# Attention score block 0 and value block 3 run over 128 columns instead of 256

## The chip, the cores and the metric

The kernel runs on one core of a Trainium2 chip. The metric is the device time of one execution in microseconds (us), where lower is better. A core has a matrix engine (PE, with the loading of its stationary operand shown apart as PEld), a vector engine (DVE), a scalar engine (ACT), GpSimd (POOL), and SyncE (SP), which here issues DMA transfers. Every matmul writes to a bank of PSUM, 512 float32 columns wide, from which DVE or ACT take the result.

## The reference

Two layers of a decoder trunk at 512 tokens and width 1024. Each layer has three parallel branches (a Mamba-2 scan, latent attention, a gated delta net), a gated merge and a feed-forward part; a final norm follows. The change lies in the attention branch:

```python
kv = (rmsnorm(ckv, kv_norm_g) @ w_ukv).reshape(Bsz, S, H, MLA_NOPE + MLA_V)   # H = 8 heads
k_nope, v = jnp.split(kv, [MLA_NOPE], axis=-1)                                # 128 + 128
...
sc = (einsum('bqhd,bkhd->bhqk', qn, k_nope) + einsum('bqhr,bkr->bhqk', qp, k_pe))
qpos = blk * MLA_QBLOCK + jnp.arange(MLA_QBLOCK)                              # 4 blocks of 128 queries
sc = jnp.where(kpos[None, :] <= qpos[:, None], sc * scale, -jnp.inf)
pr = jax.nn.softmax(sc, axis=-1)
return einsum('bhqk,bkhd->bqhd', pr, v)
```

Attention is causal, so query block t sees keys of blocks 0 to t alone, and key block kb is seen by query blocks kb to 3 alone.

## The kernel before

Everything is in one function, `hybrid_kernel`, run under a framework that takes the instructions of the loops and places them on each engine's queue; the order on an engine is not that of the source, and a few places in the source raise a priority. Each engine works through its own queue in order and waits on semaphores for the others.

Matrix products are split in two: an operand in float32 becomes a high part (type float32r, rounded) and a low part (the rest, float32r too), and a product is three float32r matmuls, high by high, high by low and low by high (`mm3`, L198 to L202). Other products of the kernel, in the Mamba-2 and delta-net branches (L779, L873, L1053, L1070 and more), use plain float32 operands, and transposes (L686, L309) pass a float32 tile through PE with an identity matrix.

Attention runs in the loop over `hp` (L586): four pairs of heads in each layer, and within a pair `j` = 0, 1. So there are 4 x 2 x 2 layers = 16 passes of the inner code:

- **Scores** (L658 to L679). For each query block t, five float32r matmuls (L663 to L667) accumulate in one bank: three for the 128 non-rotary dimensions, two for the rotary ones. Their stationary operand is 128 x 128 (the queries), their moving operand is the keys, `n = max(256, (t + 1) * P)` columns wide: 256, 256, 384 and 512. A sixth matmul in bfloat16 (L668) adds the mask over the columns from `t * P` on. For t = 0 the second 128 columns are masked keys that nothing reads afterwards; L669 narrows `n` to 128 before DVE takes the row maximum (L672), ACT the exponential (L675, L676) and DVE normalises (L677, L678).
- **Values** (L680 to L706). The probabilities are transposed by key block (L686, ten transposes a head) and split into a high and a low part. Key blocks 0 and 1 give moving operands of 512 and 384 columns. Blocks 3 and 2 share one bank of transposes and one pair of tiles, `pts`: 128 columns of zeros (written once in each layer by POOL, L578), then 128 columns of block 3, then 256 of block 2. Block 2 multiplies the last 256 columns, block 3 the first 256, that is its own 128 and the 128 zeros, and adds the result to the last 256 columns of `po`. Each block takes three float32r matmuls (L702 to L704), with the values as stationary operand, 128 x 128.

The tiles of the attention stage lie in a pool `ml` that is closed after the loop; the pool `br` of the two other branches then takes its place. Products of the other branches (L200 to L202) and further weights stand on PE's queue between the pieces of attention.

Of the kernel before, what the change touches and what calls it, by code (L numbers as in the profile page):

```python
# [11 lines left out]
F32R = mybir.dt.float32r  # L12
# [8 lines left out]
P = 128  # L21
S = 512
# [33 lines left out]
def hybrid_kernel(ctx, tc, a, out, depth=2, taps=None):  # L56
# [4 lines left out]
    def mk(pl, shape, dt, tag, bufs=None):  # L61
        return pl.tile(shape, dt, tag=tag, name=f"{tag}_{next(uid)}", bufs=bufs)
# [5 lines left out]
    def f32(ap):  # L68
        return ap.bitcast(F32)
# [197 lines left out]
    def split_act(hi, lo, src):  # L267
        with tc.high_priority(30):
            act.copy(hi, src)
            dve.tensor_tensor(lo, src, f32(hi), ALU.subtract)  # L270
# [112 lines left out]
    for ly in range(depth):  # L383
# [189 lines left out]
        q_rs = mk(sp, [P, T], F32, "qrs")  # L573
        rsq(q_rs, ps[:, :T], 1.0 / 512, EPS)

        pts = [mk(ml, [P, S], F32R, f"pt{i}") for i in range(2)]
        for x in pts:
            pool.memset(f32(x[:, :P]), 0.0)  # L578

        qpl = [mk(ml, [P, S], F32R, f"qpl{j}") for j in range(2)]  # L580
        for j in range(2):
# [4 lines left out]
        for hp in range(4):  # L586
            def q_weights():
                for k0 in (0, 2):
                    raw = mk(wp, [P, 768], F32, "wraw", 2)
                    sync.dma_start(raw.rearrange("p (k n) -> p k n", k=2),  # L590
                                   a["mla_w_uq"][ly][k0 * P : (k0 + 2) * P, hp * 384 : (hp + 1) * 384].rearrange("(k p) n -> p k n", p=P))
                    for k in range(2):
                        rv = raw[:, k * 384 : (k + 1) * 384].rearrange("p (h n) -> p h n", h=2)
                        hi = mk(wp, [P, 384], F32R, "whi")
                        lo = mk(wp, [P, 384], F32R, "wlo")
                        nv = lambda x: x[:, :256].rearrange("p (h n) -> p h n", h=2)
                        pv = lambda x: x[:, 256:].rearrange("p (h n) -> p h n", h=2)
                        act.copy(nv(hi), rv[:, :, :P])
                        act.copy(pv(hi), rv[:, :, P:])
                        dve.tensor_tensor(nv(lo), rv[:, :, :P], f32(nv(hi)), ALU.subtract)  # L600
                        dve.tensor_tensor(pv(lo), rv[:, :, P:], f32(pv(hi)), ALU.subtract)
                        yield k0 + k, hi.unsqueeze(1), lo.unsqueeze(1)

            *pq, pp = dense_F(q_weights(), tiles(384), 512, cqh, cql, tag=(ly, "q", hp))

            def head_tiles(pss, nm, c=None):
                res = []
                for ps in pss:
                    hi = mk(ml, [P, S], F32R, nm + "h", 3)
                    lo = mk(ml, [P, S], F32R, nm + "l", 3)  # L610
                    if c is None:
                        split_act(hi, lo, ps)
                    else:
                        act.mul(hi, ps, c)
                        dve.scalar_tensor_tensor(lo, ps, c, f32(hi), ALU.mult, ALU.subtract)
                    res.append((hi, lo))
                return res

            qs = head_tiles(pq, "q", scale)
            qp = mk(ml, [P, S], F32, "qp")  # L620
            act.mul(qp, pp, scale)
            qr = rope(qp)

            qd = mk(lp, [P, S], F32, "mix", 8)
            for i in range(2):
                sync.dma_start(qd[64 * i : 64 * i + 64], qr[64 * (1 - i) : 64 * (1 - i) + 64])
            qps = [mk(ml, [P, S], F32R, f"qps{j}") for j in range(2)]
            for j in range(2):
                half, other = (slice(64 * i, 64 * i + 64) for i in (j, 1 - j))
                act.copy(qps[j][half], qr[half])  # L630
                dve.tensor_tensor(qpl[j][half], qr[half], f32(qps[j][half]), ALU.subtract)
                act.copy(qps[j][other], qd[other])
            wkv = list(weights(a["mla_w_ukv"][ly], hp * 512, 512, 256))
            with tc.high_priority(30):
                ks = head_tiles(dense_F(wkv, [slice(0, P), slice(256, 256 + P)], 256, ckh, ckl), "k")

            vs = []
            for j in range(2):
                if hp % 2 == 0:
                    v2 = [mk(ml, [P, S], F32R, nm, 2) for nm in ("vh", "vl")]  # L640
                elif hp == 1:
                    v2 = [mk(lp, [P, S], F32R, f"y{e}{6 + j}") for e in "hl"]
                else:
                    v2 = [mk(ml, [P, S], F32R, f"cq{e}{j}") for e in "hl"]
                vs.append([x.rearrange("p (t n) -> p t n", t=T) for x in v2])

            def ev(t, ps):
                for j in range(2):
                    split_act(*(x[:, t, :] for x in vs[j]), ps[:, j * P : (j + 1) * P])

            vcols = lambda w: w.rearrange("p (h n) -> p h n", h=2)[:, :, P:]
            dense_T(wkv, 256, 256, ckh, ckl, ev, vcols)

            for j in range(2):
                qh, ql = qs[j]
                kh, kl = ks[j]
                pn = []
                for t in range(T):  # L658
                    n = max(256, (t + 1) * P)
                    tok = slice(t * P, (t + 1) * P)  # L660
                    ps = sm_bank()
                    o = ps[:, :n]
                    pe.matmul(o, qh[:, tok], kh[:, :n], start=True, stop=False)  # L663
                    pe.matmul(o, qh[:, tok], kl[:, :n], start=False, stop=False)
                    pe.matmul(o, ql[:, tok], kh[:, :n], start=False, stop=False)
                    pe.matmul(o, qps[j][:, tok], kps[:, :n], start=False, stop=False)
                    pe.matmul(o, qpl[j][:, tok], kph[:, :n], start=False, stop=False)  # L667
                    pe.matmul(ps[:, t * P : n], id_b, am_b[:, : n - t * P], start=False, stop=True)  # L668
                    n = (t + 1) * P  # L669
                    o = ps[:, :n]  # L670
                    mx = mk(sp, [P, 1], F32, "mx", 8)
                    dve.tensor_reduce(mx, o, AX.X, ALU.max, negate=True)  # L672
                    pt_ = mk(ml, [P, (t + 1) * P], F32, f"pn{t}", 2)
                    sm = mk(sp, [P, 1], F32, "sme", 8)
                    act.activation(mx, mx, AF.Copy, scale=q_rs[:, t : t + 1])  # L675
                    act.activation(pt_[:, :n], o, AF.Exp, bias=mx, scale=q_rs[:, t : t + 1], accum_out=sm)  # L676
                    dve.reciprocal(sm, sm)  # L677
                    dve.tensor_scalar(pt_[:, :n], pt_[:, :n], sm, None, ALU.mult)  # L678
                    pn.append(pt_)  # L679
                po = y_bank()  # L680
                for kbs in ((0,), (1,), (3, 2)):
                    ps = sm_bank()
                    n = 0
                    for kb in kbs:
                        for t in range(kb, T):
                            pe.transpose(ps[:, n : n + P], pn[t][:, kb * P : (kb + 1) * P], ident)  # L686
                            n += P
                    if len(kbs) == 1:
                        th = mk(lp, [P, n], F32R, "mix", 8)
                        tl = mk(lp, [P, n], F32R, "mix", 8)  # L690
                        split_act(th, tl, ps[:, :n])
                        parts = [(kbs[0], kbs[0] * P, 0)]
                    else:

                        th, tl = pts
                        split_act(th[:, P:], tl[:, P:], ps[:, :n])
                        parts = [(2, 2 * P, 2 * P), (3, 2 * P, 0)]
                    for kb, c0, c in parts:
                        v_h, v_l = (x[:, kb, :] for x in vs[j])
                        o = po[:, c0:]  # L700
                        w = S - c0
                        pe.matmul(o, v_h, th[:, c : c + w], start=kb == 0, stop=False)  # L702
                        pe.matmul(o, v_h, tl[:, c : c + w], start=False, stop=False)
                        pe.matmul(o, v_l, th[:, c : c + w], start=False, stop=kb == T - 1)  # L704
                yh[2 * hp + j], yl[2 * hp + j] = (mk(lp, [P, S], F32R, f"y{e}{2 * hp + j}") for e in "hl")
                split_act(yh[2 * hp + j], yl[2 * hp + j], po)  # L706
                tap(f"oT{2 * hp + j}", f32(yh[2 * hp + j]))
            if hp == 0:
                dec, ndec, beta, dtq, dsk = step_sizes()
# [762 lines left out]
```

## Time and profile before

| | |
|---|---|
| runs | 2285.59, 2286.96, 2287.45 us, median 2286.96 us |
| span of the profiled execution, first to last instruction | 2283.0 us |
| around the span, against the median | 3.96 us |
| PE busy | 2260.8 us, 99% of the span, 11822 records |
| PEld busy (beside PE) | 1867.7 us, 82% |
| DVE, ACT, POOL busy | 1648.8, 1202.1, 64.9 us |
| mean granted PE clock | 0.999 of full speed |

The profiled execution has no device time of its own on the page beside its span. A row of a group gives line, engine, operation, output and inputs, shapes, count, then busy time and the mean duration of one in ns. A row of the timeline gives start and duration in us. Matmuls overlap in the pipeline: durations of neighbours overlap, so what a matmul costs is the distance from its start to the next one's, in a run where nothing waits. The attention stage of the first layer lies at about 60 to 190 us, that of the second at about 1230 to 1340 us.

### The profile page before, as it was taken

The page shows a single profiled execution, that of the slowest core. Times are in us where ns is not written, and L with a number is a line of the kernel's source. Part 1 is how long each engine was busy: PE and PEld are TensorE (multiplying, and loading weights), DVE is VectorE, ACT ScalarE, POOL GpSimd, SP SyncE. Part 2 cuts the span into 40 slices and gives each one's busy share as a digit, 9 for nine tenths or more (in the row PEclk, how much of TensorE's full clock was granted, in tenths as well). Part 3 has the DMA queues.
Part 4 walks back from the last instruction along what each step waited for, and adds up shares of the span by engine and source line. Part 5 has one row for each costly group of instructions (what it writes and reads, how often), then busy time and mean ns, then how long its engine had stood idle before and what let it go on. Part 6 is the DMA issues. An engine that isn't in the chain of part 4 may idle for free. (4 is left out here: it accounts for less than half of the span.)

```text
span 2283.0 us, 32306 instructions
## 1 busy us (share of the span) xinstructions
PE 2260.8 (99%) x11822; PEld 1867.7 (82%) x11822; DVE 1648.8 (72%) x3250; ACT 1202.1 (53%) x2508; POOL 64.9 (3%) x83
## 2 busy tenths in 40 slices
PE   9999999999999999999999999999999999999998
PEld 8888777888888888888888888788888887888886
DVE  7777567876667778767877775678757667778668
ACT  6766654333444465554657667443335445645545
POOL 1000000000000000000010000000001000000000
PEclk9999999999999999999999999999999999999999
DMA  4223634452224243233132236344422251432231
GB/s 145 81 74 102 192 99 122 115 157 75 84 74 166 65 148 107 90 100 119 47 104 81 71 110 198 98 121 140 129 76 83 65 178 44 166 111 99 86 111 47
DMA packets 220176, 244.23 MB, mean 107 GB/s; under 512 B 34272, under 2 KB 172528, under 8 KB 220016
## 3 DMA queue, kind: packets, MB, share of 16 engines
q1 hardware_dynamic: 220016, 242.16, 34.6%
q8 instruction: 93, 1.52, 0.3%
q14 instruction: 67, 0.55, 0.1%
HBM read 225.66 MB, written 11.74 MB: 104 GB/s over the span
## 5 line engine op out<-in xcount | busy, mean ns | idle before, releaser
L172 ACT CAST whi<-wraw 128x512 fp32r<-128x512 f32 (+1 forms) x536 | 329.4, 618 | 540.4 <-PE acc L201 365.0
L173 DVE TENSOR_TENSOR wlo<-wraw,whi 128x512 fp32r<-128x512 f32 (+1 forms) x536 | 365.3, 687 | 343.6 <-ACT whi L172 334.2
L200 PE MATMUL acc<-xh,whi 128*128 128x512 f32 (+1 forms) x1344 | 525.7, 392 | 0.2 <-ACT whi L172 0.2
L202 PE MATMUL acc<-xh,wlo 128*128 128x512 f32 (+1 forms) x1344 | 520.5, 388 | 0.0
L201 PE MATMUL acc<-xl,whi 128*128 128x512 f32 (+1 forms) x1344 | 520.3, 387 | 0.0
L202 PEld LDWEIGHTS acc<-xh,wlo 128*128 128x128 f32 x1344 | 252.5, 188 | 49.2 <-DVE wlo L173 0.4
L200 PEld LDWEIGHTS acc<-xh,whi 128*128 128x128 f32 x1344 | 252.5, 188 | 48.9 <-ACT whi L172 0.6
L201 PEld LDWEIGHTS acc<-xl,whi 128*128 128x128 f32 x1344 | 252.9, 188 | 47.3 <-DVE xl L274 0.7
L172 ACT CAST whi<-wr 128x512 fp32r<-128x512 f32 x168 | 104.3, 621 | 107.8 <-PE acc L201 47.6
L200 PE MATMUL acc<-yh,whi 128*128 128x512 f32 x384 | 152.2, 400 | 0.0
L201 PE MATMUL acc<-yl,whi 128*128 128x512 f32 x384 | 150.2, 391 | 0.0
L202 PE MATMUL acc<-yh,wlo 128*128 128x512 f32 x384 | 149.8, 390 | 0.0
L173 DVE TENSOR_TENSOR wlo<-wr,whi 128x512 fp32r<-128x512 f32 x168 | 113.3, 687 | 35.3 <-ACT whi L172 34.5
L727 DVE SCALAR_TENSOR_TENSOR ckl<-acc,pc,ckl 128x511 f32<-128x511 f32 (+2 forms) x168 | 121.2, 744 | 17.9 <-ACT ckl L723 10.6
L200 PEld LDWEIGHTS acc<-yh,whi 128*128 128x128 f32 x384 | 71.5, 188 | 16.5 <-ACT yh L273 2.3
L202 PEld LDWEIGHTS acc<-yh,wlo 128*128 128x128 f32 x384 | 72.1, 188 | 15.1
L201 PEld LDWEIGHTS acc<-yl,whi 128*128 128x128 f32 x384 | 72.2, 188 | 14.2
L200 PE MATMUL acc<-whi,xh 128*128 128x512 f32 (+1 forms) x208 | 79.7, 385 | 0.0
L201 PE MATMUL acc<-wlo,xh 128*128 128x512 f32 (+1 forms) x208 | 79.3, 381 | 0.0
L202 PE MATMUL acc<-whi,xl 128*128 128x512 f32 (+1 forms) x208 | 78.9, 382 | 0.0
L486 ACT ACTIVATE eE<-eE,cum 128x128 f32<-128x128 f32 x192 | 62.6, 391 | 30.8 <-DMA eE<-d_c 26.8
L1212 DVE TENSOR_TENSOR h<-h,acc 128x512 f32<-128x512 f32 x120 | 77.1, 681 | 0.1
(462 smaller groups left out, 4542.3 us busy)
## 6 DMA issues: line engine op xcount, KB each, us to landing
wraw<-in_w_in_dram SPq DMA_DIRECT2D x144, 512.0 KB, 3.6
wraw<-in_w_up_dram SPq DMA_DIRECT2D x64, 512.0 KB, 3.6
wr<-in_w_down_dram SPq DMA_DIRECT2D x32, 1024.0 KB, 5.0
eE<-d_c SPq DMA_DIRECT2D x48, 256.0 KB, 4.3
wraw<-in_w_mla_out_dram SPq DMA_DIRECT2D x16, 512.0 KB, 3.4
eE<-d_e SPq DMA_DIRECT2D x32, 256.0 KB, 3.0
wraw<-in_w_ssd_out_dram SPq DMA_DIRECT2D x16, 512.0 KB, 3.3
wraw<-in_w_gdn_out_dram SPq DMA_DIRECT2D x16, 512.0 KB, 3.3
```

Source lines behind the costliest of these rows:

```text
L172: act.copy(hi, raw)
L173: dve.tensor_tensor(lo, raw, f32(hi), ALU.subtract)
L200: pe.matmul(o, ah, bh, start=start, stop=False, skip_group_check=more)
L201: pe.matmul(o, ah, bl, start=False, stop=False, skip_group_check=more)
L202: return pe.matmul(o, al, bh, start=False, stop=stop, skip_group_check=more)
L486: act.activation(o[:, i], o[:, i], AF.Relu, scale=-1.0, bias=cum[:, t, h0 + i : h0 + i + 1])
L727: dve.scalar_tensor_tensor(acc[:, d:], ps[:, : S - d], taps_[3 - d], acc[:, d:], ALU.mult, ALU.add)
L1212: dve.tensor_tensor(hs_, hs_, ps[t], op)
```

## The change

The first query block's scores and the fourth key block's value product lose their 128 padded columns: `n` is 128 for t = 0, for the five score matmuls and the mask's; the tiles `pts` are 384 columns wide instead of 512 and need no zeros, so POOL's two memsets a layer go; block 3 multiplies its own 128 columns and adds them to the last 128 columns of `po`. What the other engines read and write is as before.

```diff
-        pts = [mk(ml, [P, S], F32R, f"pt{i}") for i in range(2)]
-        for x in pts:
-            pool.memset(f32(x[:, :P]), 0.0)
+        pts = [mk(ml, [P, S - P], F32R, f"pt{i}") for i in range(2)]
...
-                    n = max(256, (t + 1) * P)
+                    n = (t + 1) * P
...
-                    n = (t + 1) * P
-                    o = ps[:, :n]
                     mx = mk(sp, [P, 1], F32, "mx", 8)
...
-                        split_act(th[:, P:], tl[:, P:], ps[:, :n])
-                        parts = [(2, 2 * P, 2 * P), (3, 2 * P, 0)]
+                        split_act(th, tl, ps[:, :n])
+                        parts = [(2, 2 * P, P), (3, 3 * P, 0)]
```

## The prediction

> **What bounds the kernel.** I read the page's engine table first, then the busy times by stage, then who PE waits for.
>
> ```profile
> span 2283.0 us, 32306 instructions
> PE 2260.8 (99%) x11822; PEld 1867.7 (82%) x11822; DVE 1648.8 (72%) x3250; ACT 1202.1 (53%) x2508; POOL 64.9 (3%) x83
> ```
>
> PE has 22.2 us of idle time in the whole span. The stages of attention, and the stage right behind the first of them (columns: stretch, its length, then busy time of PE, PEld, DVE, ACT, POOL, PE clock, DMA):
>
> ```profile
> 60.00:190.00 130.00, 128.72 (x728) 106.42 (x727) 100.47 (x246) 89.89 (x242) 1.01 (x1) 1.00 0.26 73
> 1230.00:1340.00 110.00, 108.74 (x596) 89.09 (x595) 85.16 (x195) 75.70 (x192) 0.00 (x0) 1.00 0.29 83
> 190.00:230.00 40.00, 40.00 (x194) 32.79 (x193) 27.39 (x44) 25.75 (x54) 0.00 (x0) 1.00 0.41 119
> ```
>
> In the 240 us of attention PE is idle for 1.28 + 1.26 = 2.5 us, at full clock. Of all PE's waits, those of the attention stage are the last row and a few like it (waiting line, releasing line, us in total, times, longest):
>
> ```profile
> PE sm L752 <- DVE ft L282: 2.0, 2, 1.6
> ...
> PE sm L686 <- DVE pn L678: 1.2, 2, 0.6
> ```
>
> So in these stages time is PE time: what the change adds to or takes from PE's queue moves the end one for one, less at most 2.5 us that could vanish in waits. Everything turns on what a 128-column float32r matmul costs.
>
> **How many matmuls are cut.** One row for each kind, grouped by shape:
>
> ```profile
> L664 PE MATMUL sm<-kl,qh 128*128 128x256 f32 x32 | 9.0, 282 | 0.0
> L702 PE MATMUL yt<-pt,vh 128*128 128x256 f32 x16 | 4.5, 281 | 0.0
> L702 PE MATMUL yt<-pt,yh 128*128 128x256 f32 x8 | 2.3, 282 | 0.0
> L702 PE MATMUL yt<-pt,cqh 128*128 128x256 f32 x8 | 2.2, 280 | 0.0
> L668 PE MATMUL sm<-am_b,id_b 128*128 128x256 bf16 x16 | 4.5, 283 | 0.0
> ```
>
> A score line has 32 records of 256 columns, 16 for t = 0 and 16 for t = 1; the first half shrinks: 5 lines x 16 = 80. A value line has 16 + 8 + 8 = 32, half of them block 3: 3 lines x 16 = 48. Together **128 float32r matmuls** go from 256 to 128 columns, with 128 stationary columns before and after. The 16 mask matmuls shrink too.
>
> **What one costs now.** The value products of blocks 2 and 3 stand in one run (start, duration):
>
> ```profile
> 87.35 0.28 PE L702 MATMUL yt<-pt,vh 128*128 128x256 f32 x1
> ...
> 88.06 0.28 PE L666 MATMUL sm<-kps,qps 128*128 128x256 f32 x1
> ...
> 90.38 0.39 PE L664 MATMUL sm<-kl,qh 128*128 128x512 f32 x1
> 90.61 0.40 PE L665 MATMUL sm<-kh,ql 128*128 128x512 f32 x1
> 90.84 0.40 PE L666 MATMUL sm<-kps,qps 128*128 128x512 f32 x1
> 91.08 0.39 PE L667 MATMUL sm<-kph,qpl 128*128 128x512 f32 x1
> ```
>
> Six 256-column matmuls stand between 87.35 and 88.06: 0.71 / 6 = **0.118 us** each. A 512-column one takes 0.70 / 3 = 0.233. The slope is (0.233 - 0.118) / 2 = 0.0575 us for 128 columns. A float32r matmul at these widths thus costs about one pass of its columns.
>
> **What one costs at 128 columns.** The trace has no float32r matmul under 256 columns, so the price is bounded from both sides.
>
> From below, streaming alone: 0.118 - 0.0575 = 0.061 us, a gain of 0.0575 x 128 = 7.4 us. A row speaks against it. Behind each short matmul the next one is late, because its 128 x 128 weights are not there yet:
>
> ```profile
> 88.91 0.28 PE L667 MATMUL sm<-kph,qpl 128*128 128x256 f32 x1
> 89.03 0.23 PE L668 MATMUL sm<-am_b,id_b 128*128 128x128 bf16 x1
> 89.07 0.42 PE L663 MATMUL sm<-kh,qh 128*128 128x384 f32 x1
> 89.33 0.34 PE L664 MATMUL sm<-kl,qh 128*128 128x384 f32 x1
> 89.50 0.34 PE L665 MATMUL sm<-kh,ql 128*128 128x384 f32 x1
> ...
> 89.03 0.20 PEld L663 LDWEIGHTS sm<-kh,qh 128*128 128x128 f32 x1
> ```
>
> The mask matmul over 128 columns ends at 89.26, the 384-column one behind it at 89.49, 0.23 later, where the same shape costs 0.17 in a run (89.33 to 89.50). Its weights began to load only when the mask matmul began: the 0.057 us that the short stream is short of a 256-column one come back as exposed load. In a run of 128-column matmuls each would expose the next one's load, and the period would be the load's, not the stream's.
>
> What the load allows, and what 128 columns of four-byte operands cost where they occur, are in two other rows, the plain float32 products and the transposes:
>
> ```profile
> 419.35 1.50 PE L873 MATMUL sm<-ft 128*128 128x128 f32 x12
> ...
> 1949.36 1.31 PE sm L309 x12
> ...
> L873 PE MATMUL sm<-ft 128*128 128x128 f32 x64 | 9.0, 278 | 0.0
> ```
>
> Twelve records of L873 take (1.50 - 0.27) / 11 = 0.112 us each, twelve transposes 1.31 / 12 = 0.109. No run of records with 128 stationary columns is faster than that, so 0.109 to 0.112 is the floor for a matmul that brings its own weights: at 0.112 the change gains (0.118 - 0.112) x 128 = 0.8 us. But L873 has 64 records, and its loop issues 2 layers x 2 units x 4 blocks x 2 = 32 products: a plain float32 product goes as two records. So a product of 128 columns of four-byte operands costs 2 x 0.112 = **0.224 us**, about four passes of its columns (4 x 0.0575 = 0.23), and nearly twice what 256 columns of float32r cost. That is the upper end: (0.224 - 0.118) x 128 = 13.6 us lost.
>
> I take the upper end. The one-pass rate is on this trace only for moving operands of 256 columns and more; every true product of four-byte operands at 128 columns pays the four-pass rate, and L873 is the nearest row in shape (128 x 128 by 128 x 128) and operand size. It is a choice: L873's operands are plain float32 and these are float32r. What makes the choice easy to live with is that the floor leaves almost nothing to win. A price still higher, four loads at 0.112, is excluded by L873 itself, which does its four passes with two.
>
> [...]
>
> **The rest of the edit.** The mask matmul (16 times): at 256 columns it starts 0.12 behind its predecessor and the next is 0.01 late; at 128 the sum of both is 0.007 less by the rows above, 0.1 us in all. Bounds 0 and 16 x 0.0575 = 0.9 us of gain; I take 0.1. POOL's memsets:
>
> ```profile
> L578 POOL MEMSET pt<- x4: 205/206/472, 23.8 to 1150.1; 128x128 f32 x4
> L269 ACT CAST pt<-sm x16: 476/486/499, 84.8 to 1324.1; 128x384 fp32r<-128x384 f32 x16
> ```
>
> About 1.1 us on an engine that is 3% busy, the first at 23.8 us for tiles first used at 84.8: nothing, hidden behind 61 us. The other offsets in `pts` move no work. Each `pts` tile is 512 bytes a partition smaller, so tiles of `br` may come to lie on others of `ml`; PE is busy for 40.00 of the 40 us from 190 to 230, so a changed wait would have to show there as idle time that is not there now. I take 0. DVE, ACT and DMA do what they did.
>
> A longer score block also delays what reads it (the row is of 60 to 190 us, eight heads):
>
> ```profile
> DVE mx L672 <- PE sm L668: 5.3, 8, 1.4
> ```
>
> Each first block would end 5 x 0.106 = 0.53 us later, and DVE, whose queue holds weight splits behind that maximum, waits so much longer in each head. In 60 to 190 us DVE has 29.5 us of slack, eight heads take 4.2. PE's own work lasts longer too, so I take 0; the bound above is that PE waits each time, 16 x 0.53 = 8.5 us. Last, the order on PE is the framework's: in the run above, scores of one head stand between value products of the one before. If it places by width, the order elsewhere may move. I give that 4 us either way, an estimate, a fifth of PE's idle time.
>
> **Sum.** +13.6 - 0.1 = +13.5 us on PE, of which I let 0.5 vanish in the waits: +13.0. The profiled span would go from 2283.0 to 2296.0; with the 3.96 us that the median stands above the span, unchanged, 2286.96 + 13.0 = **2300.0 us**, 0.57% slower. A measurement of this kernel tells about 0.2% from no change, 4.6 us.
>
> **Rivals.**
>
> *No change: one pass, bound by the load (0.25).* The float32r rate holds at 128 columns and each matmul waits for its weights: 128 x (0.112 - 0.118) = -0.8 us, with the mask 2286 us; with the load counted at 0.125, as the late matmul behind the mask suggests (89.03 plus 0.125 is where its stream would start), 2288. For it: the loads at 0.109 to 0.112 in every run. Against it: no true product at 128 columns goes in one record.
>
> *Faster: the stream decides (0.05).* If loads run ahead by more than one matmul, 128 columns cost 0.061, and the time is 2286.96 - 7.4 - 0.1 = 2279.5 us. It decides from a period under 0.082 us on (4.6 / 128 = 0.036 below 0.118). Against it: the late matmul behind the mask, and 0.109 as the shortest period anywhere with such weights. [...]
>
> *Slower still: the late maximum stalls PE (0.04).* Four passes and most of the 8.5 us: about 2308 us. Against it: the slack of DVE.
>
> That leaves 0.66 for the forecast, whose own range is 2295 to 2305 us (13.6 less 2.5 in waits, less or plus 4 for the order, cut at the ends). The range that holds 8 in 10 must reach the load-bound case: 2285 to 2305. Chances: faster 0.05, same 0.25, slower 0.66 + 0.04 = 0.70.
>
> **What would show it.** Right: in the profile after, L702 to L704 on `pt` and L663 to L667 have a 128-column form whose starts lie about 0.22 us apart, in one record or in two; PE busy in the two stages grows by about 13 us, and POOL loses four memsets. The load-bound rival: starts 0.11 to 0.12 apart, with PE's rows otherwise as they are. The streaming rival: 0.06 apart. The prediction is wrong if the period is under 0.15 us, or if a changed order on PE outweighs the 128 matmuls: then the difference lies outside the attention stages.

## The result and the profile after

The changed kernel takes 2289.61 us (median of 20 runs, 2287.58 to 2292.39) against 2285.61 us for the kernel before (20 runs, 2284.13 to 2288.06): 4.0 us slower, ratio 1.0016, 95% interval 1.0009 to 1.0022. The profiled execution spans 2285.9 us, 2.9 more than before.

The engine table and the two attention stages of the changed kernel (columns as before):

```profile
span 2285.9 us, 32289 instructions
PE 2262.4 (99%) x11822; PEld 1866.9 (82%) x11822; DVE 1650.3 (72%) x3250; ACT 1200.8 (53%) x2508; POOL 64.8 (3%) x79
```

```profile
60.00:190.00 130.00, 127.75 (x721) 104.19 (x720) 100.77 (x246) 88.50 (x242) 1.01 (x1) 1.00 0.25 70
1230.00:1340.00 110.00, 108.15 (x597) 88.61 (x596) 85.19 (x195) 77.97 (x205) 0.00 (x0) 1.00 0.29 83
```

PE has the same 11822 records, so a narrow matmul goes as one record and not as two. It is idle for 2.25 + 1.85 = 4.1 us in the attention stages, where it was idle for 2.5. (Lines have moved: L661 to L666 are the score and mask matmuls, L668 the maximum, L671 and L672 the exponential, L698 to L700 the value products.) The stretch that answers to the run of value products shown before, PE's timeline:

```profile
87.53 0.28 PE L698 MATMUL yt<-pt,vh 128*128 128x256 f32 x1
...
87.88 0.22 PE L698 MATMUL yt<-pt,vh 128*128 128x128 f32 x1
87.94 0.27 PE L699 MATMUL yt<-pt,vh 128*128 128x128 f32 x1
88.06 0.27 PE L700 MATMUL yt<-pt,vl 128*128 128x128 f32 x1
88.17 0.28 PE L663 MATMUL sm<-kh,ql 128*128 128x128 f32 x1
88.28 0.28 PE L664 MATMUL sm<-kps,qps 128*128 128x128 f32 x1
88.39 0.27 PE L665 MATMUL sm<-kph,qpl 128*128 128x128 f32 x1
88.50 0.23 PE L666 MATMUL sm<-am_b,id_b 128*128 128x128 bf16 x1
...
90.22 0.23 PE L666 MATMUL sm<-am_b,id_b 128*128 128x128 bf16 x1
90.26 0.48 PE L200 MATMUL acc<-ckh,whi 128*128 128x512 f32 x1
90.84 0.50 PE L661 MATMUL sm<-kh,qh 128*128 128x512 f32 x1
```

Two things are to be seen. The narrow matmuls start 0.11 us apart (88.06 to 88.50, four times 0.11), where 256 columns took 0.118. And the fourth score block starts at 90.84, 0.58 us behind a 512-column matmul that costs 0.23 elsewhere.

Where the 2.9 us of the profiled span went, worked out from the trace as the time from the end of one PE record to the end of the next, summed by line and width: the 256- and 128-column score and value matmuls and the masks together went from 36.37 to 34.53 us, **1.8 us less**; this sum leaves out the matmuls of 384 and 512 columns that come right behind a run of narrow ones, which the section on the order takes up. The first matmul of the fourth score block (L663 before, L661 now, 16 times) went from 4.3 to 7.8 us, **3.5 us more**; the attention transposes from 20.7 to 22.2, 1.5 more. So the matmuls gained, and waits around them took back more than that.

The wait, on both kernels at the same head. First DVE, then ACT of the kernel before, then both of the changed one:

```profile
88.62 0.29 DVE L672 TENSOR_REDUCE mx<-sm 128x1 f32<-128x128 f32 x1 [0.55 <-PE sm L668]
88.88 0.69 DVE L270 TENSOR_TENSOR yl<-yt,yh 128x512 fp32r<-128x512 f32 x1
...
89.28 0.46 ACT L676 ACTIVATE pn<-sm,mx,qrs 128x128 f32<-128x128 f32 x1
```

```profile
88.98 0.69 DVE L270 TENSOR_TENSOR yl<-yt,yh 128x512 fp32r<-128x512 f32 x1 [0.78 <-ACT yh L269]
89.59 0.61 DVE L668 TENSOR_REDUCE mx<-sm 128x1 f32<-128x128 f32 x2
...
90.23 0.46 ACT L672 ACTIVATE pn<-sm,mx,qrs 128x128 f32<-128x128 f32 x1
...
90.83 0.19 PEld L661 LDWEIGHTS sm<-kh,qh 128*128 128x128 f32 x1 [0.41 <-ACT pn L672]
```

Before, DVE takes the row maximum of the new head's first block (88.62) and then the low part of the head before (`yl`, 88.88). In the changed kernel the two have changed places on DVE's queue: the subtraction comes first, waits 0.78 us for its high part, and the maximum starts at 89.59, 0.86 after the mask matmul ended (88.73) instead of 0.04. The exponential ends a microsecond later, and only then is the bank of the first block free. There are three such banks, so the fourth score block waits for it: the weights of L661 load at 90.83, after 0.41 us of idle. In the eight second heads of the pairs the first matmul of the fourth block costs 0.58 to 0.61 us, where it cost 0.28 to 0.33.

The source says nothing about this order. It is the framework's, and it moved over the whole program.

### The profile page after: what moved, and what is told of

It is laid out like the page before. It is cut to its first block, busy times and chain, and to the rows that moved or that the text cites. A ratio compares the mean times of both kernels' runs of the same rounds, so it can differ in the third digit from the quotient of the medians.

```text
span 2285.9 us, 32289 instructions
## 1 busy us (share of the span) xinstructions
PE 2262.4 (99%) x11822; PEld 1866.9 (82%) x11822; DVE 1650.3 (72%) x3250; ACT 1200.8 (53%) x2508; POOL 64.8 (3%) x79
## 5 line engine op out<-in xcount | busy, mean ns | idle before, releaser
L201 PEld LDWEIGHTS acc<-yl,whi 128*128 128x128 f32 x384 | 72.2, 188 | 14.2
```

The lines of the kernel that those rows point to most:

```text
L201: pe.matmul(o, ah, bl, start=False, stop=False, skip_group_check=more)
```

## What a narrow matmul costs: the run widths

```diff
+    zr = mk(cst, [P, 256], F32R, "zr")
+    pool.memset(f32(zr), 0.0)
+    for i in range(24):
+        pe.matmul(warm[:, :256], zr[:, :P], zr[:, :256], start=True, stop=True)
...      # likewise 192, 128 and 64 moving columns, then 64 stationary ones with 128 and 256
```

> The kernel before, with six runs of 24 float32r matmuls on zeros added at the start, on an engine that waits for the first input there: 128 stationary columns with 256, 192, 128 and 64 moving ones, then 64 stationary columns with 128 and 256 moving ones. Theory L (the load of the stationary operand is the floor): 0.118, 0.11, 0.11 and 0.11 us each, then 0.06 and 0.11 to 0.12. Theory T (two passes of the columns under 256): 0.118, 0.17, 0.11, 0.06, then 0.11 and 0.118. Theory C (four passes under 256): 0.118, 0.34, 0.22, 0.11, then 0.22 and 0.118.

One execution, 2297.8 us, 11.6 over the median of before; the added matmuls move the plan as well, so the prices are read from the trace alone. PE's timeline, at a granted clock of 1.00 from 8 to 24 us:

```profile
8.80 3.11 PE L354 MATMUL yt<-zr 128*128 128x256 f32 x24
11.75 2.82 PE L356 MATMUL yt<-zr 128*128 128x192 f32 x24
14.41 2.81 PE L358 MATMUL yt<-zr 128*128 128x128 f32 x24
17.06 2.81 PE L360 MATMUL yt<-zr 128*128 128x64 f32 x24
19.71 1.63 PE L362 MATMUL yt<-zr 128*64 128x128 f32 x24
21.17 2.90 PE L364 MATMUL yt<-zr 128*64 128x256 f32 x24
23.90 1.47 PE L309 MATMUL sm<-ct,xr 128*128 128x128 f32 x12
```

From start to start of the groups, divided by 24: 0.123, 0.111, 0.110, 0.110 us with 128 stationary columns, then 0.061 and 0.114 with 64. With 128 stationary columns the price is flat from 192 moving columns down to 64; with the stationary operand halved, 128 moving columns take about half. Theories T and C asked for 0.17 and 0.34 us at 192 columns; both are out. So float32r stays at one pass under 256 columns, and the floor is the load of the stationary operand, 0.110 us for 128 columns. For 64 columns the run shows only that the load takes no longer than 0.061 us, since 128 moving columns need as much for themselves (0.061 us by the prediction's slope).

At 256 columns the stream (0.114 us behind the short load) is just above the load of 128 columns (0.110), so there was next to nothing to cut.

## Which half, and the order: the runs score, value, maxfirst and maxlast

**score** and **value** make one half of the change each.

```diff
-                    n = max(256, (t + 1) * P)      # score: only this
+                    n = (t + 1) * P
...
-                        parts = [(2, 2 * P, 2 * P), (3, 2 * P, 0)]      # value: only this, with pts of 384 columns
+                        parts = [(2, 2 * P, P), (3, 3 * P, 0)]
```

> The score half alone: the first score block and its mask over 128 columns, the value product of block 3 padded as before. Theory A (the order on DVE): in the plan for this kernel DVE has the first row maximum of the second head of a pair behind the low-part subtraction of the head before, so the fourth score block waits for its bank; all of the changed kernel's loss is here: about +3.5 us against before (80 matmuls at 0.105 to 0.118: -0.7; mask -0.9; stalls +3.5; the rest waits of the same kind), and the fourth score block's first matmul costs 0.58 to 0.61 us in the eight second heads. Theory B (no order, the narrow block itself): the shorter block exposes a softmax chain that PE covered before; also about +3.5. Theory C (four-pass price, the one the prediction took): +8 us.

> The value half alone: block 3's value product over 128 columns, the scores padded as before. In this kernel's plan the first maximum stays ahead of the subtraction where it was. Theories A and B: 48 matmuls at 0.105 to 0.112 instead of 0.118, -0.3 to -0.6 us against before. Theory C: +5 us.

score: 2289.99 us, before 2285.72 beside it, ratio 1.0016 (1.0007 to 1.0025). value: 2285.45, ratio 0.9999 (0.9990 to 1.0008). All of the loss is in the score half. In score the fourth block's first matmul costs 0.64 to 0.71 us in the second heads, a little more than expected; in value it costs 0.28 to 0.29, as before. Theory C is out: it asked for 8 and 5 us.

**maxfirst** gives the changed kernel the old order at this one place, **maxlast** gives the kernel before the new one.

```diff
...      # names for two instructions: first, the maximum; y_split, the subtraction
+                    if j == 1 and t == 0:
+                        after_product(y_split.ins, first.ins)     # maxfirst; maxlast: the two swapped
```

> The changed kernel with one order added: on DVE, the low-part subtraction of each pair's first head goes behind the first row maximum of the second head, as in three of four pairs before. Theory A: the fourth score block of the eight second heads no longer waits, 0.28 us instead of 0.59: 8 x 0.31 = 2.4 us less than the changed kernel, span about 2283.5. Theory B: as the changed kernel, span about 2286.

> The kernel before with the opposite order added: the first maximum of a pair's second head goes behind the subtraction of the first head, as in the changed kernel. All matmuls are as before. Theory A: the fourth score block waits in the second heads, +1.8 to +2.4 us against before, span about 2285. Theory B: no change, 2283.

maxfirst: 2287.09 us, ratio 1.0003 (0.9994 to 1.0012); the fourth block's first matmul is back at 0.28 us in all eight second heads, and of the 4.0 us of loss 1.4 remain by the medians: 2.6 are gone, where theory A had 2.4 (the rest is not of this one order). maxlast is a miss: 2286.14 us, ratio 1.0004 (0.9995 to 1.0013), not the 1.8 to 2.4 us expected. Its maximum is late (0.90 to 1.14 us behind the mask in the six second heads that had it at 0.04), but the plan, made anew around the added edge, put other products ahead of the fourth block too: in these six heads the block starts 2.2 to 2.5 us behind the first mask (1.5 before, 2.1 in the changed kernel) and costs 0.23 to 0.25 us. A late maximum before a late fourth block costs nothing here. So these two runs support theory A on one side and leave it open on the other: an added edge is a new plan, not the old one with one pair swapped.

## The order alone: the runs w248, pin_ab, pin_ba and pin_w248

**w248** changes the plan and hardly a matmul: the first score block has 248 columns.

```diff
-                    n = max(256, (t + 1) * P)
+                    n = max(248, (t + 1) * P)
```

> The kernel before with the first score block and its mask over 248 columns instead of 256: no matmul costs more than before or noticeably less (80 x 0.0036 = 0.3 us). In its plan the order on DVE is that of the changed kernel, the second heads' first maximum behind the subtraction. Theory A (the loss comes from where the plan puts things): slower than before by 2 to 5 us, with the fourth score block waiting in the second heads. Theory B (the shorter block exposes the softmax chain): as before, within 0.5 us.

2300.34 us, before 2286.14 beside it: **14.2 us slower**, ratio 1.0064 (1.0052 to 1.0077). Theory A had the direction and not the size, 2 to 5 us; eight columns fewer cost more than 128 fewer. By form, the narrow matmuls and the wait:

```profile
L664 PE MATMUL sm<-kl,qh 128*128 128x248 f32 x16 | 4.5, 279 | 0.0
L665 PE MATMUL sm<-kh,ql 128*128 128x248 f32 x16 | 4.4, 276 | 0.0
L663 PE MATMUL sm<-kh,qh 128*128 128x512 f32 x16 | 7.6, 478 | 2.2 <-ACT pn L676 1.6
L666 PE MATMUL sm<-kps,qps 128*128 128x248 f32 x16 | 5.5, 342 | 5.9 <-ACT qps L632 5.9
```

The 248-column matmuls of L664 cost 1.8 us for 16, 0.115 each, from end to end; those of L666 cost 10.1. The loss lies in waits, the largest part, some 8 us, for `qps`, the rotated queries (L632), which had not come when PE reached the product that needs them. The fourth block's first matmul takes 4.7 us more than before; the profiled execution is 18.1 us longer than that of before. For all records of L666, idle time of PE and of its weight loads taken together, w248 and then before:

```profile
L666 PE MATMUL sm<-kps,qps x64: 273/381/668, 78.8 to 1329.6; 128*128 128x248 f32 x16, 128*128 128x256 f32 x16, 128*128 128x384 f32 x16, 128*128 128x512 f32 x16
...
  ACT qps L632: 15.2, 13
```

```profile
L666 PE MATMUL sm<-kps,qps x64: 278/365/426, 77.4 to 1318.8; 128*128 128x256 f32 x32, 128*128 128x384 f32 x16, 128*128 128x512 f32 x16
...
  ACT qps L632: 1.4, 6
```

The three **pin** runs hold PE, ACT, DVE and the DMA queue of SP to a written order, instruction by instruction, by order-only edges between neighbours. pin_ab has the widths of the changed kernel in the order of before, pin_ba the widths of before in the order of the changed kernel, pin_w248 the 248 columns in the order of before.

```diff
+    for name, (n, runs) in ORDER.items():          # the order of the other kernel, for each engine
+        seq = [made[name][a + i] for a, k in runs for i in range(k)]
+        for x, y in zip(seq, seq[1:]):
+            tc.add_manual_dep(y, x.name, order_only, reason="order")
```

> The changed kernel's widths in the order of the kernel before: PE, ACT, DVE and the DMA queue of SP are each held to the order that they had before, instruction by instruction. Theory A (the loss is the plan's): 128 matmuls give 1.0 us, the mask 0.85; 1.9 us faster than before, ratio 0.9992, less what waits take back, at most 0.5. Theory B (the shorter block exposes the softmax chain): no faster than before, up to 2 us slower.

> The opposite: the widths of the kernel before, 256 columns with padding, in the order of the changed kernel. Theory A: slower than before by what the changed kernel loses and the 1.9 us that its matmuls gain, +4 to +6 us, and slower than the changed kernel. Theory B: as before.

> The first score block over 248 columns, which was 14 us slower than before in its own plan, in the order of the kernel before. Theory A: as before, -0.3 us. Theory B, or a price of the width itself: still about 14 us slower.

> The changed kernel again, beside the three others on the same chip: +4.0 us against before, as measured first.

| run, beside before at 2285.55 us | median us | ratio and interval |
|---|---|---|
| pin_ab: narrow, order of before | 2283.44 | 0.9990 (0.9982 to 0.9999) |
| pin_ba: padded, order of the changed kernel | 2289.89 | 1.0018 (1.0009 to 1.0027) |
| pin_w248: 248 columns, order of before | 2284.78 | 1.0000 (0.9991 to 1.0009) |
| again: the changed kernel | 2288.74 | 1.0015 (1.0006 to 1.0024) |

All four came out as theory A had them, by their medians. The narrow matmuls alone gain 2.1 us (0.2 to 4.1 by the interval); the order alone loses 4.3 (2.1 to 6.2); the 14.2 us of w248 are gone with its order. Theory B, that the shorter block exposes a chain whatever the order, is out: pin_ab has the shorter block and the lowest median of the study. The smaller tiles `pts`, and whatever came to lie on them, are out as a cause too: pin_ab has them and is not slower, pin_ba hasn't and is. The page of pin_ab, and the same head as above (the recording helper gives every instruction the line L77):

```profile
span 2282.0 us, 32286 instructions
...
PE 2259.0 (99%) x11822; PEld 1867.2 (82%) x11822; DVE 1649.3 (72%) x3250; ACT 1202.6 (53%) x2508; POOL 65.4 (3%) x79
```

```profile
88.04 0.27 PE L77 MATMUL sm<-kps,qps 128*128 128x128 f32 x1
88.16 0.27 PE L77 MATMUL sm<-kph,qpl 128*128 128x128 f32 x1
88.27 0.23 PE L77 MATMUL sm<-am_b,id_b 128*128 128x128 bf16 x1
88.31 0.36 PE L77 MATMUL sm<-kh,qh 128*128 128x256 f32 x1
88.51 0.28 PE L77 MATMUL sm<-kl,qh 128*128 128x256 f32 x1
...
90.03 0.47 PE L77 MATMUL sm<-kh,qh 128*128 128x512 f32 x1
...
88.54 0.29 DVE L77 TENSOR_REDUCE mx<-sm 128x1 f32<-128x128 f32 x1 [0.40 <-PE sm L77]
88.86 0.69 DVE L77 TENSOR_TENSOR yl<-yt,yh 128x512 fp32r<-128x512 f32 x1
```

The narrow matmuls are as cheap as in the changed kernel, the maximum stands ahead of the subtraction, and the fourth block starts at 90.03 with no wait. The same place on PE before, with the mask over 256 columns:

```profile
88.30 0.28 PE L668 MATMUL sm<-am_b,id_b 128*128 128x256 bf16 x1
88.34 0.37 PE L663 MATMUL sm<-kh,qh 128*128 128x256 f32 x1
88.55 0.28 PE L664 MATMUL sm<-kl,qh 128*128 128x256 f32 x1
```

PE has one order in both, so its 11822 records pair one by one, and the work can be taken apart, again from the end of one record to the end of the next. The 128 narrow matmuls take 2.0 us less than the wide ones did: the 38 that begin a run save 0.036 us each, the other 90 save 0.007. The 22 matmuls right behind a run that no mask ends take 1.0 us more, because their own load now comes late (in the changed kernel the load for the 384-column matmul at 87.12 starts 0.05 us ahead of it; before, for the same matmul at 87.00, 0.12 us). The 16 masks take 0.126 us before and 0.072 now, and the matmul behind each 0.123 before and 0.174 now: 0.85 us less and 0.82 more. Together this is 1.0 us less, and the two profiled spans, 2283.0 and 2282.0, differ by as much. The expectation of 1.9 us counted the mask's gain as kept; the median's 2.1 can't be told from 1.0 by its interval.

## Two attempts at a better kernel: the runs maxact and valuemask

**maxact** adds a second edge to maxfirst, against a wait of the first head; **valuemask** takes the value half and narrows the first mask alone.

```diff
+                        if hp == 1 and k0 == 0 and k == 0:
+                            after_product(cast.ins, ex0.ins)                             # maxact
...
-                    pe.matmul(ps[:, t * P : n], id_b, am_b[:, : n - t * P], start=False, stop=True)
+                    pe.matmul(ps[:, t * P : (t + 1) * P], id_b, am_b[:, :P], start=False, stop=True)   # valuemask
```

> The order of the run maxfirst, and on ACT the second pair's first weight cast goes behind the first exponential of each layer's first head, which was late by that cast. Theory A: the fourth score block of that head no longer costs 0.71 but 0.24 to 0.3 us, 2 x 0.4 to 0.5 = 0.8 to 1.0 us less than maxfirst. A rival (D): the fourth block then waits for the first maximum's scaling or the weights come late instead, no change against maxfirst.

> The value half of the change, and the first mask matmul over 128 columns, while the five score matmuls of the first block keep 256. The plan keeps the maximum ahead of the subtraction. By the changed kernel's rows: 48 x -0.007 = -0.3 us and -0.85 us for the mask, -1.1 us against before (0.9995). Rival: the mask's gain is only moved to the next matmul's exposed load, -0.3 us.

maxact went wrong by far: 2303.25 us, ratio 1.0073 (1.0060 to 1.0086). The new plan brings the rotary products ahead of their queries, as in w248:

```profile
L666 PE MATMUL sm<-kps,qps x64: 272/364/668, 76.5 to 1330.9; 128*128 128x128 f32 x16, 128*128 128x256 f32 x16, 128*128 128x384 f32 x16, 128*128 128x512 f32 x16
...
  ACT qps L632: 24.8, 12
```

The wait in the first head, and what follows it on PE (start, duration; then the stretch, with the granted clock as the last column but two):

```profile
76.52 0.47 PE L666 MATMUL sm<-kps,qps 128*128 128x128 f32 x1 [5.04 <-ACT qps L632]
...
78.69 0.80 PE L663 MATMUL sm<-kh,qh 128*128 128x512 f32 x1
79.29 0.63 PE L664 MATMUL sm<-kl,qh 128*128 128x512 f32 x1
79.72 0.63 PE L665 MATMUL sm<-kh,ql 128*128 128x512 f32 x1
```

```profile
75.00:80.00 5.00, 3.48 (x12) 2.88 (x13) 2.01 (x7) 3.43 (x11) 0.00 (x0) 0.50 0.06 14
```

PE waits 5.04 us, and behind the wait it runs at a granted clock of 0.50: 512 columns take 0.43 us (79.29 to 79.72) and not 0.23. So the 0.60 us that the fourth block costs here (78.69 to 79.29) don't tell whether the added edge removed its own wait. The same happens in the second layer, with 0.50 from 1215 to 1220 us. All five executions of maxact have a mean clock of 0.995 or 0.996, those of before beside them 0.998 or 0.999, so a part of this loss is the clock and not the wait itself.

valuemask: 2285.36 us, before 2286.14, ratio 0.9999 (0.9990 to 1.0008), no difference that can be told by the time. The trace settles it for the rival: the 16 first masks take 0.072 us each instead of 0.126, and the matmul behind each 0.174 instead of 0.123, so the mask's gain returns as the next matmul's late load.

## Why the prediction was wrong

- **The price of a narrow matmul**, the step that carried the sum, failed. The upper end was taken, four passes and 0.224 us, from L873, a plain float32 product. The run widths shows 0.110, and no more at 192 columns (0.111), where two passes would be 0.17: float32r keeps its one pass. The lower row, 0.109 to 0.112 from the transposes and single records, was the right one, and the late matmul behind the short mask had shown why. Nearness in shape and operand size was a bad indicator; the number of records was the better one: float32r products have one record each at 128, 256, 384 and 512 columns of the changed kernel (16 for 16 on each score line), the plain float32 products of L873 two (64 for 32).
- **The load-bound rival** had this price, the mechanism and, at the old order, the gain: 0.9 us, where pin_ab has 1.0 by the paired records and 2.1, not told from it, by the median. It missed the time, 2286 us against 2289.61, because it too left the order at nothing. A first narrow matmul in a run costs less than its flat 0.112 (87.88 to 87.94, 0.06 us), but the wide one behind the run pays most of it back (pin_ab: 38 first ones save 0.036 us each, 1.4 in all, and the 22 wide ones behind a run without a mask take 1.0 more).
- **The mask's term** held: 0.1 us was taken, and the 16 masks with the matmuls behind them went from 3.97 to 3.93 us. The runs' expectations, with 0.85 and 0.9 us, were the worse ones.
- **The streaming rival's price** holds for that first one alone. It asked for 0.061 in every one; widths has 0.110 at 64 columns.
- **The order**, taken as 0 and bounded at 4 us either way, was the term that decided the sign: 4.3 us lost at the old widths (pin_ba), 5.3 at the new (again against pin_ab), and about 14 for the 248 columns (w248 against pin_w248, whose ratio to before is 1.0000). The bound, a fifth of PE's idle time, was no bound: a new order can make idle time that was not there. For this case the prediction looked for the difference outside the attention stages; the largest wait, 3.5 us at the fourth score block, lies inside them.
- **The late maximum** was named as a place where PE could stall, by way of a longer block. The place and the waiters were right, the cause was not: the block became shorter, and the maximum was late because of what stood before it on DVE's queue.
- **Counts, memsets and cover** held: 128 narrow matmuls and 16 masks as counted, POOL at 79 instructions instead of 83 with no effect that can be told (value has none of the four memsets and a ratio of 0.9999), and DVE, ACT and DMA with the work that they had.
- **The forecast's sign** is luck: it came out for another reason than the one given, and the size, 0.16%, is within what was called no change.

What stays open is why the plan depends on the width as it does: that eight columns fewer change it is shown by w248, what rule of the framework makes it so is not. The attention transposes' 1.5 us were not taken apart.

## What to carry to other kernels

A float32r matmul whose stream is shorter than the load of its own stationary operand cost the load here: 0.110 us at 128 and 64 moving columns, with 128 stationary ones (widths). So look for the moving width at which the stream gets as long as the load, here just under 256 columns (0.114 us of stream, 0.110 of load): the 128 columns of padding cost almost nothing, and cutting them gained 1.0 us of 2283 by the records of pin_ab. A saving on one matmul counts only together with the matmul behind it: the 16 shorter masks gained 0.85 us and the matmuls behind them lost 0.82. Where a framework places the instructions, an edit can be two edits, the work and the plan; compare the order on each engine before explaining a difference, and hold the old order fixed to measure the work alone. A single added edge can be worse than the order that it mends, since the whole plan is made anew.

## What the runs showed of the hardware beside that

A float32r matmul with 64 stationary columns takes 0.061 us at 128 moving columns, about half of the 0.110 that 128 stationary ones take (widths), so it is the stationary side that prices a narrow product. A run of narrow matmuls behind a wide one starts with one at stream speed (0.06 us, 87.88 to 87.94), and the wide one behind the run is late by nearly as much: 256 columns there take 0.17 us in pin_ab and 0.12 before. A wait of 5.04 us on PE was followed by a granted clock of 0.50, at which 512 columns took 0.43 us (maxact).
